# Attention over compressed blocks: one full transpose and a 128-row values product in place of two narrow transposes and a 32-row product

## The chip, the cores and the metric

The kernel runs on one core of one Trainium2 chip. The metric is the device time of one execution in microseconds. It was measured in three runs of the kernel before, and one further execution was profiled.

## The reference, cut to what matters

One layer of a decoder block: a projection of the normalized input is split into attention inputs, a state space mixer (S5) and gates; attention and S5 are gated, summed and projected; an MLP follows. 256 tokens, 2048 channels, all in fp32. The attention has 16 heads of 128 channels in four groups that share keys and values, and three branches: compressed blocks (15 of them, padded to 16), selected blocks and a sliding window.

```python
s_c = jnp.einsum('bqgrd,bngd->bgrqn', qb, kc)
p_c = masked_softmax(s_c, cmp_end[None, :] <= t[:, None])
o_c = jnp.einsum('bgrqn,bngd->bqgrd', p_c.astype(vc.dtype), vc)
...
return gb[..., 0:1] * o_c + gb[..., 1:2] * o_s + gb[..., 2:3] * o_w
...
y_b = y_s * jax.nn.sigmoid(y_s @ w_glu[l] + b_glu[l])
```

With 256 tokens every selected block and the whole window lie within reach, so the selected and the window branch are ordinary causal attention with keys and values of their own. The change concerns `o_c`, the product of the compressed branch's probabilities with the values `vc`.

## The kernel before, in words

**The large products.** Every weight product goes through "units". A unit loads 128x1024 weights into a `raw` tile (SyncE's queue, L210), ScalarE copies them to `hi` (`copy`, L117), VectorE subtracts to `lo` (`tt`, L120), and TensorE makes three products of each 128x128 piece (hi with hi, hi with lo, lo with hi; L315, L317, L318 in `gemm_pass`). `run_units` (L226) is the planner. For each unit i it issues the loads up to seven ahead, the hi copy, then the products of the unit two before (`SPLIT = 2`), the lo split, then due small steps, and then one or more steps of the background generators listed at L1549 ff. Each generator has a first and last unit and a number of steps, which are spread evenly. The order of issue on each engine is the order in which this program writes it; nothing is reordered afterwards.

**The stage of the change** is the GLU product (`glu_units`, marks "glu" to "out"), into which ada units are woven. `ada2_pe_units` (L985) does part of the adaLN vector as 32-column matmuls (L998) into bank T3, copied to `s` by ScalarE (L1000), turned at L1007 and reduced by VectorE at L1009. The finish of each GLU piece has Tanh on ScalarE (L1273) and two VectorE steps. The projections of the stage read `RU` and write banks A0 and A1, so A2 and A3 are free for attention.

**Attention** is the background generator `attention` (L1139), 34 steps for 16 heads. `attn_setup` (L1021) loads queries, keys, values and gates on SyncE's queue beforehand, among them the compressed values `vc` (32 rows, 512 columns, L1033) into a tile that used to hold the S5 operand `k0` (read for the last time by L862).

In the step of head h the program writes, in this order: `scores(h)` (three products, L1153 to L1155, banks T0 and T12), `turn1(h-1)` (four 128x128 transposes, L1203 and L1204, into T3, one ScalarE copy), `turn2(h-1)` (two 128x128 transposes, L1211, two transposes of 32 columns, L1213, into A2, two ScalarE copies), `exps(h)` (nine small VectorE instructions that mask, find maxima and negate them, with six ScalarE exponentials between). In the next step come `weigh(h)` (masks the compressed part, sums, reciprocal, scales; L1195 is its ScalarE half) and `values(h-1)` (five products into A3, L1222 to L1226, then one VectorE step).

Each head has one tile `P` of probabilities, 128 tokens of a half by columns: 768 columns for the selected and window branches of both token halves, and 64 for the compressed branch, 32 per half (16 used, 16 zero). The turned tile `PT` has 32 rows in its last 256 columns: tokens of half 0, then half 1. The product L1224 multiplies these 32 rows with the 32 rows of `vc`; all other products of `values` have 128 rows.

An fp32 product shows as two matmul records in the trace, a transpose as one. The profile names the tiles by region: `P`, `PT`, `m` and the attention inputs all lie in `RX`; `A` are the banks A0 to A3; `T` the others.

Of the kernel before, what the change touches and what calls it, by code (L numbers as in the profile page):

```python
# [81 lines left out]
def block_kernel(ctx, tc, cst_in, x, c, w_ada, b_ada, g_mix, w_in, w_ck2, pe_ck,  # L82
# [3 lines left out]
    nc = tc.nc  # L86
    V, A, PE = nc.vector, nc.scalar, nc.tensor
# [7 lines left out]
    def bank(tag):  # L95
        return pp_.tile([128, 512], FT, tag=tag, name=tag)
# [10 lines left out]
    def region(tag, n):  # L107
        return rp.tile([128, n], FT, tag=tag, name=tag)

    def scratch(name, shape):  # L110
        return dp.tile(shape, FT, tag=name, name=name)
# [4 lines left out]
    def copy(out, in_, scale=1.0):  # L116
        A.activation(out=out, in_=in_, func=AF.Copy, scale=scale)  # L117
# [10 lines left out]
    def stt(out, a, s, b, op0, op1):  # L128
        V.scalar_tensor_tensor(out=out, in0=a, scalar=s, in1=b, op0=op0, op1=op1)  # L129
# [7 lines left out]
    ident = cst[:, 0:128]  # L137
# [38 lines left out]
    d_vc = scratch("d_vc", [32, 512])  # L176
# [842 lines left out]
    at = {}  # L1019

    def attn_setup():  # L1021
        r = region("RX", 16384)
        at["r"] = r
        at["q"] = r[:, 0:4096].rearrange("p (h t) -> p h t", h=16)
        at["v"] = r[:, 4096:6144].rearrange("p (t s n) -> p t s n", t=2, s=2)
        at["K"] = r[:, 6144:8256].rearrange("p (g n) -> p g n", g=4)
        at["m"] = r[:, 8256:12352].rearrange("p (h t) -> p h t", h=16)
        at["free"] = r[:, 12352:16384]
        for i, n in enumerate(("tA", "tB")):
            at[n] = region(f"RB{i}", 4096).rearrange("p (h t) -> p h t", h=16)  # L1030
        nc.sync.dma_start(out=at["K"][:, :, 0:16], in_=d_kc.rearrange("p (g n) -> p g n", g=4))
        vc = cp.tile([128, 512], FT, tag="k0", name="vc")
        nc.sync.dma_start(out=vc[0:32], in_=d_vc)  # L1033
        at["vc"] = vc.rearrange("p (g n) -> p g n", g=4)
        for g in range(4):
            hs_ = slice(4 * g, 4 * g + 4)
            nc.sync.dma_start(out=at["q"][:, hs_, :], in_=d_q[:, hs_, :])
            for s in range(2):
                nc.sync.dma_start(
                    out=at["K"][:, g, 16:528].rearrange("p (t s n) -> p t s n", t=2, s=2)[:, :, s, :],  # L1040
                    in_=d_k[:, 4 * s + g, :].rearrange("p (t n) -> p t n", t=2))
            yield
            nc.sync.dma_start(out=at["v"][:, :, :, 128 * g:128 * g + 128], in_=d_v[:, :, :, 128 * g:128 * g + 128])
            nc.sync.dma_start(out=at["tA"][:, hs_, :], in_=d_g[:, hs_, :])
            yield
            yield
# [91 lines left out]

    def attention():  # L1139
        fa = at["free"]  # L1140
        P = [fa[:, 832 * i:832 * i + 832] for i in range(2)]
        PT = [fa[:, 1664:2688]] * 2
        sm = [fa[:, 2688 + 32 * i:2720 + 32 * i] for i in range(2)]
        for i in range(2):
            V.memset(P[i][:, 768:832], 0.0)
        q, K, vv, m = at["q"], at["K"], at["v"], at["m"]

        S = {}
# [9 lines left out]
        def exps(h):  # L1158
            S0, S1 = S["s"]
            p, s_ = P[h % 2], sm[h % 2]  # L1160
            mx, nm, su, mb = s_[:, 0:6], s_[:, 6:12], s_[:, 12:18], s_[:, 18:20]
# [20 lines left out]
        def weigh(h):  # L1182
            p, s_ = P[h % 2], sm[h % 2]
            su, cf = s_[:, 12:18], s_[:, 20:26]
            pc = p[:, 768:832].rearrange("p (i n) -> p i n", i=2)
            tt(pc[:, :, 0:16], pc[:, :, 0:16], okm, OP.mult)
            V.tensor_reduce(out=su.rearrange("p (i b) -> p i b", i=2)[:, :, 0], in_=pc[:, :, 0:16], axis=AX.X, op=OP.add)
            ts(su, su, 1e-30, OP.max)
            V.reciprocal(out=cf, in_=su)
            tt(cf.rearrange("p (i b) -> p i b", i=2), cf.rearrange("p (i b) -> p i b", i=2),  # L1190
               gates[:, :, 3 * h:3 * h + 3], OP.mult)
            for i in range(2):
                ts(pc[:, i, 0:16], pc[:, i, 0:16], cf[:, 3 * i:3 * i + 1], OP.mult)
            for s in range(2):
                A.activation(out=p[:, 128 * s:128 * s + 128], in_=p[:, 128 * s:128 * s + 128], func=AF.Copy,  # L1195
                             scale=cf[:, 1 + s:2 + s])
                ts(p[:, 256 + 256 * s:512 + 256 * s], p[:, 256 + 256 * s:512 + 256 * s], cf[:, 4 + s:5 + s], OP.mult)

        def turn1(h):
            p, o = P[h % 2], PT[h % 2]  # L1200
            ps = bank("T3")
            for s in range(2):
                PE.transpose(ps[:, 256 * s:256 * s + 128], p[:, 128 * s:128 * s + 128], ident)  # L1203
                PE.transpose(ps[:, 256 * s + 128:256 * s + 256], p[:, 256 + 256 * s:384 + 256 * s], ident)  # L1204
            copy(o[:, 0:512], ps)

        def turn2(h):
            p, o = P[h % 2], PT[h % 2]
            ps = bank("A2")
            for s in range(2):  # L1210
                PE.transpose(ps[:, 128 * s:128 * s + 128], p[:, 384 + 256 * s:512 + 256 * s], ident)  # L1211
            for i in range(2):
                PE.transpose(ps[0:32, 256 + 128 * i:384 + 128 * i], p[:, 768 + 32 * i:800 + 32 * i], ident)  # L1213
            copy(o[:, 512:768], ps[:, 0:256])
            copy(o[0:32, 768:1024], ps[0:32, 256:512])

        def values(h):
            g = h // 4
            o = PT[h % 2]
            ps = bank("A3")  # L1220
            hd = slice(128 * g, 128 * g + 128)
            PE.matmul(out=ps[:, 0:256], lhsT=vv[:, 0, 0, hd], rhs=o[:, 0:256], start=True, stop=False, skip_group_check=True)  # L1222
            PE.matmul(out=ps[:, 0:256], lhsT=vv[:, 0, 1, hd], rhs=o[:, 256:512], start=False, stop=False, skip_group_check=True)
            PE.matmul(out=ps[:, 0:256], lhsT=at["vc"][0:32, g, :], rhs=o[0:32, 768:1024], start=False, stop=False, skip_group_check=True)  # L1224
            PE.matmul(out=ps[:, 128:256], lhsT=vv[:, 1, 0, hd], rhs=o[:, 512:640], start=False, stop=False, skip_group_check=True)
            PE.matmul(out=ps[:, 128:256], lhsT=vv[:, 1, 1, hd], rhs=o[:, 640:768], start=False, stop=True, skip_group_check=True)  # L1226
            stt(m[:, h, :], at["tA"][:, h, :], 1.0, ps[:, 0:256], OP.add, OP.mult)

        for h in range(NH + 1):
            if h < NH:  # L1230
                scores(h)
            if h:
                turn1(h - 1)
                turn2(h - 1)
            if h < NH:
                exps(h)
            yield
            if h < NH:
                weigh(h)
            if h:  # L1240
                values(h - 1)
            yield
# [264 lines left out]
    with tc.manual_schedule():  # L1507
# [39 lines left out]
        def at_(name, f, nxt):  # L1547
# [16 lines left out]
            dict(name="mat1", gen=s5_matrices(1), start=marks["gb"] + CM0, end=marks["gb"] + CM1, total=4, tick=True),  # L1564
            dict(name="outs", gen=s5_outputs(), start=at_("gb", SCAN_END, "glu") + 1, end=marks["glu"] - 1, total=17),
            dict(name="load", gen=attn_setup(), start=marks["glu"] + AS0, end=marks["glu"] + AS1, total=13),
            dict(name="tb", gen=load_tb(), start=marks["glu"] + TB0, end=marks["glu"] + TB1, total=4, tick=True),
            dict(name="attn", gen=attention(), start=marks["glu"] + ATTN_WAIT, end=marks["out"] - 2, total=34),
        ]
        run_units(bgs)  # L1570
# [47 lines left out]
```

## Time and profile before

| | |
|---|---|
| median of three runs | 1780.44 us |
| lowest and highest run | 1776.47 and 1782.63 us |
| profiled execution, its own time | 1776.92 us |
| span of that execution | 1775.1 us |
| mean granted TensorE clock | 0.989 |

The span runs from the first to the last instruction of the profiled execution. PE is TensorE's matmuls, PEld its weight loads, DVE VectorE, ACT ScalarE, POOL GpSimd, SP SyncE. A duration of a matmul reaches from its start to its end in a pipeline, so durations overlap, and the distance of two starts is what a matmul costs in a stream. "Idle before" is the time in which an engine had nothing running, with the instruction that ended it; "issue" means that nothing in the profile released it.

### The profile page before, as it was taken

The page shows a single profiled execution, that of the slowest core. Times are in us where ns is not written, and L with a number is a line of the kernel's source. Part 1 is how long each engine was busy: PE and PEld are TensorE (multiplying, and loading weights), DVE is VectorE, ACT ScalarE, POOL GpSimd, SP SyncE. Part 2 cuts the span into 40 slices and gives each one's busy share as a digit, 9 for nine tenths or more (in the row PEclk, how much of TensorE's full clock was granted, in tenths as well). Part 3 has the DMA queues.
Part 4 walks back from the last instruction along what each step waited for, and adds up shares of the span by engine and source line. Part 5 has one row for each costly group of instructions (what it writes and reads, how often), then busy time and mean ns, then how long its engine had stood idle before and what let it go on. Part 6 is the DMA issues. An engine that isn't in the chain of part 4 may idle for free.

```text
span 1775.1 us, 37647 instructions
## 1 busy us (share of the span) xinstructions
PE 1718.9 (97%) x15710; PEld 1620.6 (91%) x15710; DVE 1108.5 (62%) x2032; ACT 856.3 (48%) x1379; POOL 29.4 (2%) x51
## 2 busy tenths in 40 slices
PE   6999999999999999999999999999999999999997
PEld 4788898789999988888899999999999999999997
DVE  4868468347888966666656575555555555565554
ACT  3433443754333477655544454444444544464444
POOL 1000000300000000000000000000000000000000
PEclk8999999999999999999999999999999999999998
DMA  9988756858888867876667567777777565556662
GB/s 349 327 275 315 260 180 206 267 160 296 274 274 283 254 211 243 296 244 211 214 198 262 176 219 235 235 227 224 240 234 227 179 183 184 181 176 184 184 181 81
DMA packets 121802, 406.26 MB, mean 229 GB/s; under 512 B 13904, under 2 KB 18480, under 8 KB 120864
## 3 DMA queue, kind: packets, MB, share of 16 engines
q1 hardware_dynamic: 114480, 385.49, 67.1%
q10 hardware_dynamic: 5408, 9.75, 1.5%
q0 software_dynamic: 1744, 8.62, 1.4%
q8 instruction: 123, 2.02, 0.4%
q14 instruction: 47, 0.39, 0.1%
HBM read 384.84 MB, written 16.88 MB: 226 GB/s over the span
## 4 chain that ended last, share of the span: by engine, by line
PE 87%; DVE 5%; ACT 4%; DMA 2%; issue 1%; ACTq 0%; SPq 0%; DVEq 0%
PE A L315 25%; PE A L317 24%; PE A L318 24%; PE T L998 2%; DVE lo L120 2%; PE T L343 2%; ACT hi L117 1%; ACT RX L117 1%; DMA raw<-in_l_ada_dram 1%; PE T L809 1%; PE A L897 1%; DMA raw<-in_l_vals_dram 1%; PE A L899 1%; PE A L898 1%; PE T L737 0%
## 5 line engine op out<-in xcount | busy, mean ns | idle before, releaser
L120 DVE TENSOR_TENSOR lo<-raw,hi 128x1024 fp32r<-128x1024 f32 (+1 forms) x497 | 607.0, 1223 | 507.8 <-ACT hi L117 504.0
L117 ACT ACTIVATE hi<-raw 128x1024 fp32r<-128x1024 f32 (+1 forms) x497 | 523.1, 1055 | 580.5 <-PE A L317 539.0
L315 PE MATMUL A<-RU,hi 128*128 128x256 f32 x2560 | 740.2, 289 | 3.3 <-ACT hi L117 1.5
L318 PE MATMUL A<-RU,lo 128*128 128x256 f32 x2560 | 728.0, 284 | 1.5 <-DVE lo L120 1.5
L317 PE MATMUL A<-RU,hi 128*128 128x256 f32 x2560 | 727.8, 284 | 0.0
L315 PEld LDWEIGHTS A<-RU,hi 128*128 128x128 f32 x2560 | 494.3, 193 | 27.7 <-issue 20.9
L318 PEld LDWEIGHTS A<-RU,lo 128*128 128x128 f32 x2560 | 494.4, 193 | 2.0 <-DVE lo L120 1.9
L317 PEld LDWEIGHTS A<-RU,hi 128*128 128x128 f32 x2560 | 494.7, 193 | 0.3 <-DVE RU L129 0.2
L315 PE MATMUL A<-RB,hi 128*128 128x256 f32 x1280 | 363.9, 284 | 1.4 <-ACT RB L117 1.2
L317 PE MATMUL A<-RB,hi 128*128 128x256 f32 x1280 | 362.6, 283 | 0.2
L318 PE MATMUL A<-RB,lo 128*128 128x256 f32 x1280 | 362.2, 283 | 0.0
L315 PEld LDWEIGHTS A<-RB,hi 128*128 128x128 f32 x1280 | 245.7, 192 | 3.4 <-ACT RB L117 1.6
L317 PEld LDWEIGHTS A<-RB,hi 128*128 128x128 f32 x1280 | 245.7, 192 | 0.6 <-DVE RB L129 0.5
L318 PEld LDWEIGHTS A<-RB,lo 128*128 128x128 f32 x1280 | 245.6, 192 | 0.0
L117 ACT ACTIVATE RB<-RX 128x256 fp32r<-128x256 f32 x160 | 64.3, 403 | 27.4 <-DVE RX L129 27.4
L120 DVE TENSOR_TENSOR RX<-A,RX 128x512 f32<-128x512 f32 x60 | 40.4, 687 | 30.2 <-PE A L318 29.2
L129 DVE SCALAR_TENSOR_TENSOR s<-raw,cond,s 128x1024 f32<-128x1024 f32 x45 | 57.6, 1279 | 0.1
L117 ACT ACTIVATE RX<-T 128x256 f32<-128x256 f32 (+2 forms) x81 | 39.8, 638 | 35.8 <-PE T L1204 26.6
L120 DVE TENSOR_TENSOR RB<-RX,RB 128x256 fp32r<-128x256 f32 x128 | 53.4, 418 | 1.6 <-ACT RB L117 1.6
L343 PE MATMUL T<-raw,cond 128*32 128x256 f32 x512 | 40.8, 413 | 10.0 <-DMA raw<-in_l_ada_dram 10.0
L998 PE MATMUL T<-raw,cond 128*32 128x128 f32 x1280 | 43.2, 276 | 2.0 <-ACT RX L117 2.0
L998 PEld LDWEIGHTS T<-raw,cond 128*32 128x32 f32 x1280 | 32.5, 109 | 8.4 <-ACT RX L117 4.2
(237 smaller groups left out, 1248.1 us busy)
## 6 DMA issues: line engine op xcount, KB each, us to landing
raw<-in_l_ada_dram SPq DMA_DIRECT2D x144, 512.0 KB, 4.9
raw<-in_w_in_dram SPq DMA_DIRECT2D x144, 512.0 KB, 4.6
raw<-in_w_up_dram SPq DMA_DIRECT2D x128, 512.0 KB, 4.2
raw<-in_w_down_dram SPq DMA_DIRECT2D x128, 512.0 KB, 4.5
raw<-in_w_ada_dram SPq DMA_DIRECT2D x48, 512.0 KB, 4.1
raw<-in_w_glu_dram SPq DMA_DIRECT2D x32, 512.0 KB, 5.1
raw<-in_w_out_dram SPq DMA_DIRECT2D x32, 512.0 KB, 5.8
raw<-in_l_keys_dram SPq DMA_DIRECT2D x16, 512.0 KB, 4.4
```

Source lines behind the costliest of these rows:

```text
L117: A.activation(out=out, in_=in_, func=AF.Copy, scale=scale)
L120: V.tensor_tensor(out=out, in0=a, in1=b, op=op)
L129: V.scalar_tensor_tensor(out=out, in0=a, scalar=s, in1=b, op0=op0, op1=op1)
L315: PE.matmul(out=o, lhsT=w.hi[:, at], rhs=xh, start=first and j % 2 == 0, stop=False, skip_group_check=True)
L317: PE.matmul(out=o, lhsT=w.hi[:, at], rhs=xl, start=False, stop=False, skip_group_check=True)
L318: PE.matmul(out=o, lhsT=w.lo[:, at], rhs=xh, start=False, stop=last, skip_group_check=True)
L343: PE.matmul(out=ps[q:q + 32, :], lhsT=cond[:, t0 + t:t0 + t + 1].to_broadcast([128, 32]), rhs=r[:, t, :], start=t0 == 0, stop=t0 == 12, ti ...
L809: PE.matmul(out=ps[h][:, (w * 2 + r_) * 128:(w * 2 + r_) * 128 + 128], lhsT=bl[c4 // 2][64 * h:64 * h + 64, (gw + w) % 16, r_, :], rhs=stk ...
L897: PE.matmul(out=o, lhsT=xh, rhs=u.hi[:, at], start=kt == 0, stop=False)
L898: PE.matmul(out=o, lhsT=xl, rhs=u.hi[:, at], start=False, stop=False)
L899: PE.matmul(out=o, lhsT=xh, rhs=lo[:, at], start=False, stop=kt == 15)
L998: PE.matmul(out=ps[q:q + 32, 0:128], lhsT=cond[:, kt:kt + 1].to_broadcast([128, 32]), rhs=r[:, kt % 8, :], start=kt < 4, stop=kt >= 12, ti ...
```

## The change

The compressed values are loaded twice, into rows 0 to 31 and rows 32 to 63 of `vc`, and the other rows are set to zero. `P` gets 64 more zero columns, so that its last 128 columns can be turned by one full transpose. Of the result, rows 0 to 31 hold half 0's probabilities and rows 32 to 63 half 1's. ScalarE copies the former to columns 768 to 895 of `PT`, and VectorE the latter to rows 32 to 63 of columns 896 to 1023; the rest of these 256 columns was set to zero once. The product with `vc` then has 128 rows. The VectorE copy is written at the end of `turn2`, ahead of `exps` of the next head.

```diff
         vc = cp.tile([128, 512], FT, tag="k0", name="vc")
-        nc.sync.dma_start(out=vc[0:32], in_=d_vc)
+        nc.gpsimd.memset(vc, 0.0)
+        for i in range(2):
+            nc.sync.dma_start(out=vc[32 * i:32 * i + 32], in_=d_vc)
...
-        P = [fa[:, 832 * i:832 * i + 832] for i in range(2)]
-        PT = [fa[:, 1664:2688]] * 2
-        sm = [fa[:, 2688 + 32 * i:2720 + 32 * i] for i in range(2)]
+        P = [fa[:, 896 * i:896 * i + 896] for i in range(2)]
+        PT = [fa[:, 1792:2816]] * 2
+        sm = [fa[:, 2816 + 32 * i:2848 + 32 * i] for i in range(2)]
         for i in range(2):
-            V.memset(P[i][:, 768:832], 0.0)
+            V.memset(P[i][:, 768:896], 0.0)
+
+        V.memset(PT[0][:, 768:1024], 0.0)
...
             for s in range(2):
                 PE.transpose(ps[:, 128 * s:128 * s + 128], p[:, 384 + 256 * s:512 + 256 * s], ident)
-            for i in range(2):
-                PE.transpose(ps[0:32, 256 + 128 * i:384 + 128 * i], p[:, 768 + 32 * i:800 + 32 * i], ident)
+            PE.transpose(ps[:, 256:384], p[:, 768:896], ident)
             copy(o[:, 512:768], ps[:, 0:256])
-            copy(o[0:32, 768:1024], ps[0:32, 256:512])
+            copy(o[0:32, 768:896], ps[0:32, 256:384])
+            V.tensor_copy(out=o[32:64, 896:1024], in_=ps[32:64, 256:384])
...
-            PE.matmul(out=ps[:, 0:256], lhsT=at["vc"][0:32, g, :], rhs=o[0:32, 768:1024], start=False, stop=False, skip_group_check=True)
+            PE.matmul(out=ps[:, 0:256], lhsT=at["vc"][:, g, :], rhs=o[:, 768:1024], start=False, stop=False, skip_group_check=True)
```

## Rows read from the trace of the kernel before

**Rows 1.** The page's first part: busy time of each engine, its share of the span and its instructions.

```profile
PE 1718.9 (97%) x15710; PEld 1620.6 (91%) x15710; DVE 1108.5 (62%) x2032; ACT 856.3 (48%) x1379; POOL 29.4 (2%) x51
```

**Rows 2.** TensorE's waits between 705 and 905 us: the waiting line, who ended the wait, us in total, times, the longest.

```profile
PE T L998 <- ACT RX L117: 2.0, 8, 0.3
PE T L1203 <- ACT RX L1195: 1.4, 1, 1.4
PE A L1222 <- ACT RX L117: 1.0, 3, 0.5
PE T L1007 <- ACT s L117: 0.7, 1, 0.7
```

**Rows 3.** TensorE in order of time, the values product of head 10 and what follows it: start, length, engine, line, operation.

```profile
834.14 0.60 PE L1222 MATMUL A<-RX 128*128 128x256 f32 x2
834.57 0.59 PE L1223 MATMUL A<-RX 128*128 128x256 f32 x2
835.10 0.69 PE L1224 MATMUL A<-RX,vc 32*128 32x256 f32 x2
835.72 0.49 PE L1225 MATMUL A<-RX 128*128 128x128 f32 x2
836.05 0.39 PE L1226 MATMUL A<-RX 128*128 128x128 f32 x2
836.27 0.62 PE L1153 MATMUL T<-RX 128*128 128x272 f32 x2
```

**Rows 4.** Weight loads of the values products between 720 and 905 us, grouped by line: count, busy time, mean ns of one, idle time before them and its releasers.

```profile
L1226 PEld LDWEIGHTS A<-RX 128*128 128x128 f32 x32 | 5.1, 201 | 0.0
L1225 PEld LDWEIGHTS A<-RX 128*128 128x128 f32 x32 | 5.0, 195 | 5.6 <-issue 5.6
L1224 PEld LDWEIGHTS A<-RX,vc 32*128 32x128 f32 x32 | 4.9, 190 | 5.6 <-issue 5.0 <-ACT RX L1174 0.7
```

**Rows 5.** TensorE in order of time, the end of the turn of head 10 and what follows it.

```profile
837.95 0.27 PE L1204 MATMUL T<-cst,RX 128*128 128x128 f32 x1
...
838.27 0.38 PE L1213 MATMUL A<-cst,RX 128*32 128x128 f32 x2
838.91 1.08 PE L998 MATMUL T<-raw,cond 128*32 128x128 f32 x32 [0.25 <-ACT RX L117]
```

**Rows 6.** Groups by line and form: ScalarE's copy of the compressed part, and VectorE's one copy of 128x128 out of PSUM.

```profile
L117 ACT ACTIVATE RX<-A 32x256 f32<-32x256 f32 x16 | 5.8, 361 | 0.0
...
L440 DVE COPY cols<-A 128x128 f32<-128x128 f32 x1 | 0.3, 291 | 4.7 <-PE A L439 4.7
```

**Rows 7.** VectorE, ScalarE and TensorE in order of time from 850 to 890 us, those rows that mark the steps. VectorE's rows are the first step of exps of heads 12, 13, 14 and 15. ScalarE's: the first instruction behind the exponentials of heads 12 and 13 (854.43, 863.19), the scaling of weigh of heads 12, 14 and 15 (L1195), the last read of the exponentials of head 15 (885.00). TensorE's: the 32-column transposes that end the turn of heads 11, 13 and 14 (L1213), the first transpose of the turn of heads 12 to 15 (L1203).

```profile
850.19 0.45 DVE L120 TENSOR_TENSOR T<-T,cst 128x272 f32<-128x272 f32 x1 [1.02 <-PE T L1153]
859.02 0.44 DVE L120 TENSOR_TENSOR T<-T,cst 128x272 f32<-128x272 f32 x1
873.33 0.44 DVE L120 TENSOR_TENSOR T<-T,cst 128x272 f32<-128x272 f32 x1
881.43 0.44 DVE L120 TENSOR_TENSOR T<-T,cst 128x272 f32<-128x272 f32 x1
...
854.43 0.25 ACT L117 ACTIVATE s<-T 128x128 f32<-128x128 f32 x1
857.94 0.69 ACT L1195 ACTIVATE RX<-RX 128x128 f32<-128x128 f32 x2 [2.31 <-DVE RX L120]
863.19 0.25 ACT L117 ACTIVATE s<-T 128x128 f32<-128x128 f32 x1
880.35 0.69 ACT L1195 ACTIVATE RX<-RX 128x128 f32<-128x128 f32 x2 [2.31 <-DVE RX L120]
885.00 0.21 ACT L1178 ACTIVATION_READ_ACCUMULATOR RX<-T,RX 128x1 f32 x1
888.46 0.69 ACT L1195 ACTIVATE RX<-RX 128x128 f32<-128x128 f32 x2 [2.31 <-DVE RX L120]
...
851.54 0.38 PE L1213 MATMUL A<-cst,RX 128*32 128x128 f32 x2
859.64 0.27 PE L1203 MATMUL T<-cst,RX 128*128 128x128 f32 x1
873.27 0.33 PE L1203 MATMUL T<-cst,RX 128*128 128x128 f32 x1 [0.20 <-DVE ada L1009]
873.98 0.38 PE L1213 MATMUL A<-cst,RX 128*32 128x128 f32 x2
880.81 0.33 PE L1203 MATMUL T<-cst,RX 128*128 128x128 f32 x1
881.63 0.38 PE L1213 MATMUL A<-cst,RX 128*32 128x128 f32 x2
889.72 0.27 PE L1203 MATMUL T<-cst,RX 128*128 128x128 f32 x1
```

**Rows 8.** One stretch of the table by windows: from and to, its length, busy us (and instructions) of PE, PEld, DVE, ACT, POOL, the granted clock of TensorE, DMA share, GB/s.

```profile
740.00:760.00 20.00, 19.48 (x139) 16.44 (x137) 14.44 (x43) 11.36 (x37) 0.00 (x0) 0.83 0.59 197
```

**Rows 9.** GpSimd's memsets of 128x1024 in a group; SyncE's issue of the load of `vc`, in order of time; and the wait of the issue behind it, from the waits of SyncE's queue between 690 and 725 us.

```profile
L698 POOL MEMSET s<- 128x1024 f32 x2 | 1.9, 962 | 43.9 <-DVE RX L120 43.9
...
709.84 0.69 SPq L1033 DMA_DIRECT2D vc<-d_vc  x1
...
SPq L1037 <- DMA raw<-in_w_glu_dram: 1.9, 1, 1.9
```

## The prediction, as it was put on record before the changed kernel ran

> **What bounds the kernel now.** I read the page's busy times first, then TensorE's waits in the stage that the change touches (about 720 to 900 us of the span), then that stage in order of time on each engine. TensorE is busy for 97% of the span, VectorE for 62% [rows 1]. So a stop or a saved slot on TensorE moves the end, unless ScalarE or VectorE are late in that place. TensorE's longest waits in the stage [rows 2] are few, some 5 us in 200, but they decide this case: eight of the ada products and three of the values for ScalarE's copy of the turned probabilities, one of 1.4 us for the weighing (L1195), one for the staged ada sums (L1007).
>
> **The values product.** Five products per head go to bank A3. In head 10 they start at 834.14, 834.57, 835.10, 835.72 and 836.05, and the next work starts at 836.27 [rows 3]. Two products of the same width with 128 rows follow each other after 0.43 us (834.14 to 834.57). The step into the 32-row product takes 0.53, the step out of it 0.62, and the 128-wide L1225 takes 0.33 where L1226 takes 0.22. That is 0.10 + 0.19 + 0.11 = 0.40 us per head above an even row of products. The cause shows in the weight loads: those of L1224 and L1225 stand idle for 5.6 us each over 16 heads, 0.35 at each border, with no releaser but "issue" [rows 4]; a load of 128 rows behind a product of 128 rows has no such gap (L1226, 0.0). With 128 rows in L1224 both borders vanish, while the matmul itself streams the same 256 columns. So **-0.40 us per head, 16 x 0.40 = -6.4 us gross**.
>
> [...]
>
> **The turn.** Two transposes of 32 columns become one of 128. Three of 128 columns start within 0.32 us (837.95 to 838.27), and two of 32 last 0.38 together where one transpose lasts 0.27 [rows 5]: 0.11 apart in either width. So 0.11 us per head leaves TensorE, 1.8 us gross. But in eleven heads the next instruction behind the turn waits for ScalarE's copy of the first four transposes (838.91, 0.25 us idle, one of eight; three more at L1222 [rows 2, 5]); there the slot only becomes waiting. Five heads (0, 2, 13, 14, 15) go on with projections: -0.55 us gross.
>
> **The copies.** ScalarE's copy of 32x256 (361 ns [rows 6]) becomes 32x128; that relieves it of between nothing and half, and I take nothing, as no step below waits for it. VectorE gets a new copy of 32x128 out of PSUM; its nearest row is 128x128 out of PSUM, 291 ns [rows 6]. By itself 16 x 0.29 = 4.7 us on an engine that is busy 62% of the span. What matters is its place: it stands in the queue **ahead of exps(h)**, and it waits for the turn of head h-1. Until now exps(h) waited only for scores(h), which TensorE does before the turn. Behind the copy are queued the nine steps of exps(h), then the lo split of the next unit, then weigh(h). ScalarE's exponentials wait for exps, its hi copy and Tanh stand behind those, and the turn of head h waits for weigh(h).
>
> Where VectorE comes late to exps(h) the copy costs its own 0.2 to 0.3 us. Where VectorE comes early, it now waits for the last transpose. Exps takes 3.78 us from its first step to ScalarE's last (881.43 to 885.21 [rows 7]). From the last transpose's start to the first step of exps I take 0.51, an estimate: 0.27 for the transpose and 0.24 for the signal and most of the copy; the ends are 0.27 (the copy costs nothing) and 0.27 + 0.29 + 0.1.
>
> In the middle of the stage this is mostly absorbed: VectorE is early in heads 5, 6, 7, 10, 11 and 12 (there 850.19 against a turn that ends behind 851.54 [rows 7]), its exponentials end some 1.3 us later, but before the next turn both engines wait for TensorE again (the idle VectorE has ahead of scores, such as 1.02 us at 850.19 [rows 7]). It is not absorbed in these places:
> - **Start, to 739.17.** TensorE waits 1.4 us there for the weighing of head 1 [rows 2]. The larger memsets (three of 128 to 256 columns instead of two of 64; by the copy of 128 columns, 291 ns [rows 6], between 0 and 0.9 more; I take 0.3, as a memset reads nothing) and the first copy (0.2) lie on that chain: +0.5, and what head 0 saved is lost.
> - **Heads 7 and 9.** The L1007 wait of 0.7 [rows 2] hangs on exps(8): +0.2, and the turn of head 8 follows its weighing without slack, so head 7's 0.40 is lost. The turn of head 10 follows its weighing as closely as that of head 12 does (below); the 1.3 us use that up, so head 9's 0.40 is lost too.
> - **Heads 11 to 15**, worked out from [rows 7], each "now" to "then", on one scale that starts at 850 (the full transpose starts where the first narrow one did):
>  exps(12) 850.19 to 851.54 + 0.51 = 852.05; the exponentials end at 855.8 instead of 854.4, so the weighing goes from 857.94 to 859.34, and the turn needs 0.46 behind that (880.35 to 880.81): 859.80 against 859.64. Head 11's 0.40 is gone.
>  exps(13) 859.02 to 859.80 + 0.71 + 0.51 = 861.0 (0.71 from the first to the last transpose, as at 873.27 to 873.98); the exponentials end at 864.7 instead of 863.2, +1.5. From here ScalarE and VectorE run in a chain to the reduce that frees the bank for the turn (its releaser at 873.27): 873.27 to 874.77.
>  exps(14) 873.33 to 873.98 + 1.5 + 0.51 = 875.99, +2.66; weighing 880.35 to 883.01, turn 880.81 to 883.47.
>  exps(15) 881.43 to 881.63 + 2.66 + 0.51 = 884.80, +3.37; weighing 888.46 to 891.83, turn 892.28 instead of 889.72: +2.56. With head 15's own 0.40 + 0.11 the stage leaves this part at **+2.05**.
>
> **Setup.** One memset of 128x512 on GpSimd: by the row 128x1024, 962 ns, about 0.5 us [rows 9]. Its tile is last read by L862, in the stage before, and GpSimd's queue is empty, so it is done before SyncE reaches the load at 709.8. One more load of 64 KB costs SyncE an issue of 0.69 us; the issue behind it waits 1.9 us for a weight transfer anyway [rows 9]. Behind it stand the loads of queries, keys and values and the weights. Ends: 0 (within that wait) and +0.69 (all of it reaches the weights); I take 0, as the nearest row is that wait.
>
> **Sum.** Values of heads 1 to 6, 8, 10: 8 x 0.40 = -3.2; turn of head 2: -0.1; start +0.5; head 8 +0.2; heads 11 to 15 +2.05: **-0.55 us**. Behind the stage TensorE is the bound again, so the shift is carried to the end. The sum stands against the profiled execution's 1776.92 us (span 1775.1), giving 1776.4. That execution lies 3.5 us below the median of the three runs shown (1780.44), so for the median I say 1779.9. A measurement of this kernel can tell about 0.3%, 5.3 us, from no change.
>
> **Rivals.**
> *The copy is covered* (0.23). If VectorE's wait does not reach TensorE at all, the gross gains stay: -6.4 - 0.55, less head 0 (0.51) and the +0.5 of the start: -5.9, that is 1774.5, faster by over 0.3%. For it: SPLIT lets two units lie between the split and its product, and TensorE hardly waits in the middle. Against it: the last five heads have no slack in the rows.
> [...]
> [...]
>
> **How the numbers follow.** The forecast with one clock stretch more or less has 0.55, the rivals 0.23, 0.13 and 0.05, and 0.04 is left for what I don't see. Faster by over 0.3% (below 1775.1): 0.23, the covered case. Slower (above 1785.8): 0.13 and half of the rest, 0.15. Within: 0.62. The range takes in the covered case at 1774.5 and reaches to 1786, where the forecast with one stretch more and the load's 0.69 us (1784.0) still lies inside and the second stretch does not; the runs shown spread over 6 us themselves.
>
> **What would show it.** Right: in the profile after, L1224 has no "issue" idle and the five products of a head take 1.73 us instead of 2.13; the new VectorE copy stands behind PE's turn in the waits with 5 to 10 us in all; TensorE has new waits of over 1 us at L1007 or L1203 near 871 to 885. [...]

## The result, and the profile after

The changed kernel takes **1788.67 us** (median of five runs, 1787.38 to 1791.06), the kernel before 1780.44 beside it (five runs, 1776.47 to 1782.63). The ratio is 1.0053 with an interval of 1.0037 to 1.0070: slower by 0.53%, some 9.4 us (the medians lie 8.2 us apart). The forecast was no difference, with 1779.9 us; the time lies above its range, which reached to 1786.

The profiled execution took 1791.06 us, with a span of 1789.3 and a mean granted clock of 0.984. Before the stage of the change begins, it is already 5.5 us later than the one of before (first product of the scores at 727.23 against 721.71). That lateness is older than the change: the last product of the stage before (L862) starts at 702.8 against 697.4, and the change's memset and loads come behind it (703.2 and 715.4). From that product to the first scores it is 24.3 us before and 24.4 after, and 24.3 to 24.6 in all nine kernels of this study. So I compare the stage alone, from the first scores to the values product of the last head:

| kernel | to the scores of pass 12 | from there to the last values | stage | ratio to before |
|---|---|---|---|---|
| before | 127.82 | 43.93 | 171.75 | |
| changed | 130.19 | 50.34 | 180.53 | 1.0053 |
| e1 copy behind exps | 127.99 | 42.88 | 170.87 | 0.9999 |
| e2 both copies on ScalarE | 123.95 | 43.58 | 167.53 | 0.9983 |
| e3 full rows only | 123.81 | 43.18 | 166.99 | 0.9974 |
| e4 VectorE's copy only | 129.13 | 49.61 | 178.74 | 1.0046 |
| e5 copy out of bank A3 | 128.33 | 47.58 | 175.91 | 1.0032 |
| e6 copies without a wait | 124.94 | 43.83 | 168.77 | 0.9986 |
| e7 copy out of a bank of the scores | 127.31 | 48.41 | 175.72 | 1.0022 |

(Stages are of one execution each, in us; ratios are of repeated runs, and 0.001 is 1.8 us.) A stage also holds what its execution lost to a lower granted clock, an estimate from the table of windows of 20 us (in each, 20 us times what the granted clock lacks to 1.00): 3.4 us before, 5.2 changed, 1.8 in e1, e2 and e6, 0 in e3 and e4, 3.4 in e5, 3.6 in e7; so the ratios decide, and the stages show where. The stage grew by 8.8 us, 6.4 of them in the last four heads. Behind it nothing changes: from the last values to the end of the span it is 881.6 us before and 881.5 after.

The values product did what was forecast. In order of time on TensorE, the same product as in [rows 3] (with the heads counted from 0 it is that of head 9, there called head 10):

```profile
840.58 0.60 PE L1226 MATMUL A<-RX 128*128 128x256 f32 x2
841.01 0.59 PE L1227 MATMUL A<-RX 128*128 128x256 f32 x2
841.44 0.59 PE L1228 MATMUL A<-RX,vc 128*128 128x256 f32 x2
841.87 0.38 PE L1229 MATMUL A<-RX 128*128 128x128 f32 x2
842.10 0.39 PE L1230 MATMUL A<-RX 128*128 128x128 f32 x2
842.32 0.62 PE L1157 MATMUL T<-RX 128*128 128x272 f32 x2
```

From 840.58 to 842.32 it is 1.74 us, where 2.13 were. The idle time of the weight loads at the two borders, 5.6 us each in [rows 4], is down to 1.5 and 1.1 in the groups by line, 725 to 911 us, near the 1.0 of a border between two full products (L1227):

```profile
L1229 PEld LDWEIGHTS A<-RX 128*128 128x128 f32 x32 | 6.7, 208 | 1.1
L1227 PEld LDWEIGHTS A<-RX 128*128 128x128 f32 x32 | 6.3, 198 | 1.0
L1228 PEld LDWEIGHTS A<-RX,vc 128*128 128x128 f32 x32 | 6.3, 201 | 1.5 <-DVE RX L1219 0.6
```

What took the gain and more is in TensorE's waits, 705 to 920 us, the answer to [rows 2]:

```profile
PE T L1207 <- ACT RX L1199: 7.0, 4, 2.5
PE T L1007 <- ACT s L117: 4.9, 3, 2.2
PE T L998 <- ACT RX L117: 2.9, 8, 0.4
PE A L1226 <- ACT RX L117: 1.4, 3, 0.6
PE T L1207 <- ACT s L117: 1.3, 1, 1.3
```

The turn's wait for the weighing (L1207, formerly L1203) rose from 1.4 to 7.0 us, the one at L1007 from 0.7 to 4.9. Behind both stands one line of VectorE's waits, 720 to 920 us, and it names ScalarE, not TensorE. Before, the wait ahead of exps was one for the scores; the first line is of before, the second of the changed kernel:

```profile
DVE T L120 <- PE T L1153: 2.9, 3, 1.0
...
DVE RX L1219 <- ACT RX L117: 15.7, 10, 2.8
```

The second is the new copy. Pass 12 in order of time shows it, TensorE's last two transposes, then ScalarE, then VectorE, the place of [rows 7] at 850.19:

```profile
859.20 0.38 PE L1215 MATMUL A<-cst,RX 128*128 128x128 f32 x2
859.42 0.27 PE L1216 MATMUL A<-cst,RX 128*128 128x128 f32 x1
...
859.40 0.60 ACT L117 ACTIVATE RX<-T 128x512 f32<-128x512 f32 x1 [3.03 <-PE T L1208]
859.90 0.52 ACT L117 ACTIVATE RX<-A 128x256 f32<-128x256 f32 x2
...
860.45 0.28 DVE L1219 COPY RX<-A 32x128 f32<-32x128 f32 x1 [2.82 <-ACT RX L117]
860.76 0.45 DVE L120 TENSOR_TENSOR T<-T,cst 128x272 f32<-128x272 f32 x1
```

The last transpose is over at 859.69. VectorE's copy starts at 860.45, when ScalarE's two copies out of the same bank have ended (859.90 + 0.52 = 860.42). From the last transpose's start to the first step of exps it is 860.76 - 859.42 = **1.34 us**, and so it is in heads 13, 14 and 15 (869.23 to 870.57, 885.05 to 886.39, 895.14 to 896.48). The prediction took 0.51. The written program says why: this copy waits for two engines there. In e7 (below), which reads another bank into the same place, it waits for one.

```
changed  L1219 COPY RX<-A  32x128  waits PE, Activation
e7       L1221 COPY RX<-T  32x128  waits PE
```

So the program keeps these two engines apart at bank A2, though both only read it; the trace agrees in that VectorE's copy starts 0.03 us behind the end of ScalarE's second copy (860.45 against 860.42). What this wait is for, and what happens when two engines do read the bank at once, no run here shows.

The clock, from the table by windows, the answer to [rows 8]: from and to, length, busy us (and instructions) of PE, PEld, DVE, ACT, POOL, the granted clock, DMA share, GB/s.

```profile
740.00:760.00 20.00, 17.07 (x107) 15.08 (x106) 14.76 (x43) 10.93 (x33) 0.00 (x0) 0.91 0.66 217
800.00:820.00 20.00, 17.54 (x171) 15.89 (x172) 13.33 (x39) 10.80 (x35) 0.00 (x0) 0.98 0.63 234
820.00:840.00 20.00, 19.28 (x204) 17.10 (x204) 12.03 (x43) 8.87 (x30) 0.00 (x0) 0.94 0.60 204
880.00:900.00 20.00, 15.17 (x92) 13.62 (x93) 12.34 (x45) 9.64 (x32) 0.56 (x1) 0.91 0.58 202
```

Three stretches at a lower level in place of one: in windows of 1 us the granted clock is 0.50 from 748 to 750, from 820 to 822 and from 895 to 897, and before from 742 to 748. By the windows of 20 us that is an estimated 20 x (0.09 + 0.02 + 0.06 + 0.09) = 5.2 us lost, where before lost 20 x 0.17 = 3.4. Each of the three follows a stop of TensorE of over 2 us (2.30 us up to 745.41, 2.10 up to 817.61, 2.50 up to 893.88); one of 2.24 us, up to 882.05, is followed by none (1.00 from 882 to 893).

### The profile page after: what moved, and what is told of

The parts are those of the page before. It is cut to its first block, busy times and chain, and to the rows that moved or that the text cites. A ratio compares the mean times of both kernels' runs of the same rounds, so it can differ in the third digit from the quotient of the medians.

```text
span 1789.3 us, 37647 instructions
## 1 busy us (share of the span) xinstructions
PE 1719.8 (96%) x15694; PEld 1626.3 (91%) x15694; DVE 1114.0 (62%) x2049; ACT 855.7 (48%) x1379; POOL 30.0 (2%) x52
## 4 chain that ended last, share of the span: by engine, by line
PE 85%; DVE 6%; ACT 5%; DMA 3%; issue 1%; ACTq 0%; SPq 0%; DVEq 0%
PE A L315 25%; PE A L317 24%; PE A L318 24%; DVE lo L120 2%; PE T L998 2%; PE T L343 1%; ACT hi L117 1%; ACT RX L117 1%; DMA raw<-in_l_ada_dram 1%; PE T L809 1%; PE A L897 1%; DMA raw<-in_l_vals_dram 1%; PE A L899 1%; PE A L898 1%; PE T L867 1%
## 5 line engine op out<-in xcount | busy, mean ns | idle before, releaser
L117 ACT ACTIVATE hi<-raw 128x1024 fp32r<-128x1024 f32 (+1 forms) x497 | 523.1, 1055 | 579.7 <-PE A L317 540.2
L117 ACT ACTIVATE RB<-RX 128x256 fp32r<-128x256 f32 x160 | 64.3, 403 | 27.4 <-DVE RX L129 27.4
L117 ACT ACTIVATE RX<-T 128x256 f32<-128x256 f32 (+2 forms) x81 | 39.7, 636 | 25.4 <-PE T L1208 15.7
```

## The experiments

The theories, in the order in which they came up. A, the place: VectorE's copy stands ahead of exps and waits, and that delays the exponentials and the next turn. B, the work: it is the added time on VectorE and ScalarE. C, the clock: new stops of TensorE that bring more stretches at the lower level, or a fuller product that brings the clock down. Behind the first four runs A was narrowed, and in the expectations of e5 and e7 it says: what the prediction lacked is the wait for ScalarE's copies in the same bank, and its wait for the transposes was sized rightly. Its rival D says: the place ahead of exps costs the most of it, even if the copy waits for the transposes alone.

**e1, the copy behind exps.** Written in `late(h - 1)`, called after `exps(h)`:

```diff
+            S["c"] = ps
+
+        def late(h):
+            o, ps = PT[h % 2], S["c"]
             V.tensor_copy(out=o[32:64, 896:1024], in_=ps[32:64, 256:384])
...
+            if h:
+                late(h - 1)
```

> The changed kernel with VectorE's new copy written behind exps of the next head instead of ahead of it; all else stays. Theory A (the place of the copy in VectorE's queue is the cause: it waits for ScalarE's two copies out of the same bank, ends 1.34 us behind the last transpose's start, and exps, hi, lo, weigh and the next turn follow): the values product keeps its 1.73 us per head, TensorE's waits in the stage fall from 18.4 us back to 5 to 7, and the kernel is 5 to 7 us faster than the one before the change: ratio 0.996 to 0.998. Rival B (the work that was added costs: VectorE's 16 x 0.28 us, the memsets, the second load): nothing of that is gone, so it stays near 1.005. Rival C (TensorE's clock falls because of the fuller product): it stays at or above 1.003 with granted clocks below 1.00 in the stage.

Measured: 0.9999 (0.9990 to 1.0008), 1778.52 us. The loss is gone, so the place carries it. The gain that was expected is missing, and the waits of TensorE show where it went:

```profile
PE A L1232 <- DVE RX L1223: 4.0, 3, 2.4
PE A L1232 <- issue: 1.5, 1, 1.5
```

In heads 0 to 3 the values product (L1232 is the product with `vc` here) follows so soon that it stands for the copy, which now comes late: 4.0 us in three heads, and 1.5 in head 0, where the profile names no releaser but the copy ends at 734.14 and the product starts at 734.24.

**e2, both copies on ScalarE.** No copy on VectorE.

```diff
-            V.tensor_copy(out=o[32:64, 896:1024], in_=ps[32:64, 256:384])
+            copy(o[32:64, 896:1024], ps[32:64, 256:384])
```

> The changed kernel with the second copy of the compressed part on ScalarE too, so VectorE has no copy there; ScalarE makes 256, 128 and 128 columns instead of 256 and 256. Theory A: 5 to 6 us faster than the kernel before (ratio 0.997), a little behind the copy on VectorE behind exps, as ScalarE has some 0.25 us more per head. Rival B, if VectorE's added work is the cost: about 4 us of the 8 come back, ratio 1.002 to 1.003. Rival C: at or above 1.003.

Measured: 0.9983 (0.9973 to 0.9993), 1775.23 us: a gain of 3.0 us, less than the 5 to 6 that were expected and about half of what the prediction's covered case gave (5.9 us).

**e3, full rows only.** To the kernel before: `vc` and the last columns of `PT` are zeroed, and the product reads 128 rows; the narrow transposes and ScalarE's one copy stay.

```diff
+        nc.gpsimd.memset(vc, 0.0)
...
+        V.memset(PT[0][:, 768:1024], 0.0)
...
-            PE.matmul(out=ps[:, 0:256], lhsT=at["vc"][0:32, g, :], rhs=o[0:32, 768:1024], start=False, stop=False, skip_group_check=True)
+            PE.matmul(out=ps[:, 0:256], lhsT=at["vc"][:, g, :], rhs=o[:, 768:1024], start=False, stop=False, skip_group_check=True)
```

> The kernel before with one part of the change alone: the product with the compressed values has 128 rows, rows 32 to 127 of both operands are set to zero once; the two narrow transposes and ScalarE's one copy stay, VectorE has no copy. Theory A: the product gains 0.40 us per head, less what waits for ScalarE and VectorE anyway: 5 to 6.5 us faster, ratio 0.9965 to 0.997. Rival C (the 128-row product itself costs, by clock or by weight loads that are not hidden): 1.000 or above.

Measured: 0.9974 (0.9963 to 0.9986), 1773.29 us, the fastest of all, ahead of both kernels; 4.6 us, a little less than expected. Over these runs the mean granted clock was 0.9884, and 0.9878 in the kernel before, so some 1 us of the 4.6 may be the clock; in the two profiled stages it is 3.4 of 4.8. TensorE in order of time, the product of [rows 3] again, and then the groups of the weight loads, 720 to 905 us:

```profile
832.31 0.60 PE L1224 MATMUL A<-RX 128*128 128x256 f32 x2
...
834.05 0.62 PE L1155 MATMUL T<-RX 128*128 128x272 f32 x2
```

```profile
L1227 PEld LDWEIGHTS A<-RX 128*128 128x128 f32 x32 | 6.1, 190 | 0.8
L1226 PEld LDWEIGHTS A<-RX,vc 128*128 128x128 f32 x32 | 6.1, 190 | 0.8
```

1.74 us for the five products and 0.8 us of idle at either border, with nothing changed but the rows: the 32 rows were what cost 0.40 us per head on TensorE. In that form the block-diagonal tile is not needed; zeros below the 32 rows do.

**e4, VectorE's copy only.** To the kernel before: ScalarE copies half of the compressed part and VectorE the other half, in the place of the change, still 32 rows.

```diff
-            copy(o[0:32, 768:1024], ps[0:32, 256:512])
+            copy(o[0:32, 768:896], ps[0:32, 256:384])
+            V.tensor_copy(out=o[0:32, 896:1024], in_=ps[0:32, 384:512])
```

> The kernel before with VectorE's copy alone: ScalarE copies half 0 of the compressed part and VectorE half 1, in the place where the change has it, ahead of exps; the 32-row product and the narrow transposes stay. Theory A: the whole loss without the gain, 8 + 6 = 14 us slower, ratio 1.006 to 1.009; TensorE's waits in the stage 15 us or more. Rival B (VectorE's own 0.28 us per head, the rest being setup): under 4.5 us, ratio below 1.0025. Rival C: no change.

Measured: 1.0046 (1.0032 to 1.0060), 1786.9 us. Below what was expected, because I had added the parts up (the change's loss and the gain that it hides): the copy alone costs as much as the whole change. The waits of VectorE, then those of TensorE:

```profile
DVE RX L1216 <- ACT RX L117: 16.3, 10, 3.2
```

```profile
PE T L1203 <- ACT RX L1195: 5.3, 5, 2.1
PE T L1007 <- ACT s L117: 3.5, 3, 1.7
```

The same waits as in the changed kernel. And the clock is not needed for it: the stage takes 7.0 us longer than before with the granted clock at 1.00 in every 20 us from 720 to 900, though before lost 3.4 us there to the lower level.

**e5, the copy out of bank A3.** The full transpose is written a second time, into A3, and VectorE reads there.

```diff
+            pd = bank("A3")
+            PE.transpose(pd[:, 0:128], p[:, 768:896], ident)
...
-            V.tensor_copy(out=o[32:64, 896:1024], in_=ps[32:64, 256:384])
+            V.tensor_copy(out=o[32:64, 896:1024], in_=pd[32:64, 0:128])
```

> The changed kernel, with the full transpose of the compressed part done twice, the second time into bank A3, from which VectorE's copy reads; in the written program this copy then waits for TensorE alone and no longer for ScalarE's two copies out of A2. Its place ahead of exps stays. Theory A (what was missing in the prediction is the wait for ScalarE's copies, 0.83 us per pass: 1.34 instead of 0.51 us from the last transpose's start to exps): the stage from the first scores to the last values takes 171 to 174 us as the recorded sum has it (before 171.75, changed 180.53), ratio 0.999 to 1.001; VectorE's waits at the copy fall from 15.7 us to 5 to 9. Rival D (the place alone is the cause, the wait for the transposes is enough): the stage stays above 177 us and the ratio at 1.003 or above.

Measured: 1.0032 (1.0021 to 1.0043), 1783.94 us. By the ratio that is what was said for D (1.003 or above), by the stage, 175.91, for neither; and the run doesn't decide, as A3 is the bank of the values product, which now waits for the copy in its turn, 3.1 us:

```profile
PE A L1228 <- DVE RX L1221: 3.1, 3, 1.5
```

**e6, copies without a wait.** As e2, but in the copy's place VectorE makes two copies of the same size from a constant into columns that nothing reads.

```diff
-            V.tensor_copy(out=o[32:64, 896:1024], in_=ps[32:64, 256:384])
+            copy(o[32:64, 896:1024], ps[32:64, 256:384])
+            V.tensor_copy(out=at["free"][0:32, 2944:3072], in_=cst[0:32, 0:128])
+            V.tensor_copy(out=at["free"][0:32, 3072:3200], in_=cst[0:32, 0:128])
```

> The changed kernel with both copies of the compressed part on ScalarE (as measured above, 0.9983), and in the place of VectorE's copy two copies of 32x128 of a constant into an unused part of the region, which wait for nothing. Theory A (it is the wait, not VectorE's time): 0 to 1.5 us over 0.9983, ratio 0.998 to 0.9995; TensorE's waits in the stage as there. Rival B (VectorE's occupied time counts): 16 x 0.4 us come on top, ratio 1.001 or above.

Measured: 0.9986 (0.9976 to 0.9996), 1776.65 us, against e2's 0.9983: twice 207 ns per head on VectorE, in that very place, cost nothing that can be measured (the copy that they stand for takes 284 ns). Theory B falls.

**e7, the copy out of a bank of the scores.** As e5, but the second transpose goes into the last 128 columns of the bank that the next scores wrote just before, which no ScalarE copy of the turn reads.

```diff
+            pd = S["s"][0] if h < NH - 1 else bank("T0")
+            PE.transpose(pd[:, 384:512], p[:, 768:896], ident)
...
+            V.tensor_copy(out=o[32:64, 896:1024], in_=pd[32:64, 384:512])
```

> As the run with the copy's own bank, but the second full transpose goes into the unused columns of the bank of the scores (T0) instead of A3, so that the values product doesn't wait for VectorE's copy to give A3 back (3.1 us of TensorE's waits there). VectorE's copy stays ahead of exps and waits for TensorE alone. Theory A (the recorded chain of waits is right and only its step from the last transpose to exps was too short: 0.51 against 1.34 us): with a step of 0.6 to 0.7 us and 0.11 us per head for the second transpose, the stage takes 171 to 174 us (before 171.75, changed 180.53, copy's own bank 175.91), ratio 0.999 to 1.001. Rival D (the place ahead of exps costs more than that chain says, whatever it waits for): 175 us or more, ratio 1.002 or above.

Measured: 1.0022 (1.0013 to 1.0031), 1782.12 us, stage 175.72: just inside what was said for D (1.002 and 175 or more), outside what was said for A. So the wait for ScalarE is not the whole. Pass 12 in order of time, TensorE and VectorE, then VectorE's wait at the copy:

```profile
856.54 0.27 PE L1218 MATMUL T<-cst,RX 128*128 128x128 f32 x1
...
856.86 0.28 DVE L1221 COPY RX<-T 32x128 f32<-32x128 f32 x1 [2.20 <-PE T L1218]
857.17 0.45 DVE L120 TENSOR_TENSOR T<-T,cst 128x272 f32<-128x272 f32 x1
```

```profile
DVE RX L1221 <- PE T L1218: 9.5, 9, 2.2
```

Without ScalarE in the bank the step takes 857.17 - 856.54 = 0.63 us instead of 1.34, and more than half of the loss is gone (3.9 us are left of 9.4). What stays is the wait for the transposes. So the ratios split the change in three: without any wait (e6) 0.9986, that is -2.5 us; the wait for the transposes (e7 less e6) 0.0036, +6.4 us, of which e7's own second transposes may be up to 16 x 0.11 = 1.8; the wait for ScalarE's copies (the change less e7) 0.0031, +5.5 us. In all +9.4. By the intervals of the ratios each of the two differences is uncertain by some 2 to 3 us.

The last difference is not the wait alone. The mean granted clock was 0.985 over the runs of the change and 0.988 over those of e6 and of e7; at 1.8 us for a thousandth up to 4.7 of the 5.5 us can have gone through the clock. What the traces show without it is the step: 1.34 - 0.63 = 0.71 us in each of heads 12 to 15, some 2.8 us. How much of the rest is the lower level behind the longer stops stays open.

## Why the prediction was wrong, by its own steps

**The step that failed: "From the last transpose's start to the first step of exps I take 0.51", with ends of 0.27 and 0.66.** It measured 1.34, outside both ends. I counted what the copy waits for among the instructions that write its source, and not those that read the same bank. With a bank to itself it is 0.63, inside the ends, and the estimate would have stood. The 0.83 too few come back in each of heads 12 to 15: 4 x 0.83 = 3.3 us on a chain that the prediction had traced rightly (exps, exponentials, weighing, turn). It gave these heads +2.05, which is +2.45 up to the start of the last values, as head 15's own product comes behind it; the stretch from the scores of pass 12 to there grew by 50.34 - 43.93 = 6.4. Of the 4.0 between, 3.3 are this step, and the stretch at the lower clock near 895 is 1.8; together they are a little more than is to be explained, and I can't part them further. By the ratios the wait in the bank is worth +5.5 us with the clock's share in it (above), where the sum had 0.

**"Mostly absorbed" in the middle.** The forecast had +0.2 at L1007 near head 8 and nothing for head 3. In the profile after, in order of time, TensorE stands at both places, and longer than forecast at the start:

```profile
745.41 0.33 PE L1207 MATMUL T<-cst,RX 128*128 128x128 f32 x1 [2.30 <-ACT RX L1199]
...
767.25 0.33 PE L1207 MATMUL T<-cst,RX 128*128 128x128 f32 x1 [1.34 <-ACT s L117]
...
817.61 0.66 PE L1007 MATMUL T<-cst,s 128*128 128x128 f32 x4 [2.10 <-ACT s L117]
```

2.30 where 1.38 + 0.5 was said, 1.34 where nothing was, 2.10 where 0.7 + 0.2 was. The late exponentials delay ScalarE's copy of the ada sums (`s`, L117), which is queued behind them.

**The tail, ahead of the turns of heads 13 and 14: right in place, too small in size.** Stops of about 1.7 us were forecast near 871 and 882, which is near 879 and 890 here, as pass 12 begins 7.9 us later. Ahead of the turn of head 13 there are 2.24 (at L1007, the ada transposes just before it) and 0.28, ahead of that of head 14 there are 2.50: each some 0.8 more than forecast, about the missing 0.83 of the step. A stop of 1.11 ahead of the turn of head 12 was not named:

```profile
868.41 0.33 PE L1207 MATMUL T<-cst,RX 128*128 128x128 f32 x1 [1.11 <-ACT RX L1199]
882.05 0.66 PE L1007 MATMUL T<-cst,s 128*128 128x128 f32 x4 [2.24 <-ACT s L117]
884.34 0.33 PE L1207 MATMUL T<-cst,RX 128*128 128x128 f32 x1 [0.28 <-DVE ada L1009]
893.88 0.33 PE L1207 MATMUL T<-cst,RX 128*128 128x128 f32 x1 [2.50 <-ACT RX L1199]
```

**The values product, -0.40 us per head: right** as a price on TensorE (1.74 against 2.13). The chance of 0.05 was for a full load that waits as well, and that is out: the loads of L1228 have 1.5 us of idle in all, 0.6 of it behind the copy, in place of the 5.6.

**The covered case, -5.9 us: too much.** Free of the wait, e2, e3 and e6 gain 3.0, 4.6 and 2.5 us. The table shows where a part of the rest stays: in the last four heads these kernels take 43.58, 43.18 and 43.83 against 43.93, a gain of 0.1 to 0.75 us, where the case had counted 0.40 for each of four products and 0.11 for each of three turns, 1.9 in all. There the turn follows the weighing without slack, by the prediction's own [rows 7]; a shorter product on TensorE only lengthens the wait for ScalarE and VectorE (ahead of the turn of head 14 TensorE waits 0.81 us for the weighing in e2, 0.48 in e3 and 0.84 in e6, where it waited for nothing before). The case ought to have left heads 11 to 14 out. Where the remainder stays is not shown.

**Waiting for the transposes: about right.** The prediction's sum and its covered case lie 5.35 us apart; e7 and e6 lie 6.4 apart, with e7's own second transposes in it. It is the larger of the two waits by the ratios, as D had it, and the sum had counted it.

So against the sum of -0.55: the bank's wait +5.5, the smaller gain of the case without a wait +3.4 (1.8 of it in the last four heads), and +1.05 on the wait for the transposes make the +9.4 that were measured.

**The clock: one part, whose size stays open.** The chance of 0.13 was for two more stretches at the lower level, of 3.4 us each, and the range left room for one. No run shows that a new stop costs 3.4 us: in the stage of the profiled execution there are two stretches more, but all three are shorter, an estimated 1.6 to 1.8 us each and together 1.8 us more than before. Over the five runs the mean granted clock was 0.984 to 0.987; in the sets of e1 to e4 the kernel before had 0.985 to 0.991. A thousandth of the span is 1.8 us, so up to some 5 us of the loss could go through the clock, in the stage or out of it. What speaks against the clock as the cause is e4, which loses 8.2 us with 1.00 throughout the stage of its profiled execution and a mean of 0.985 to 0.989 over its runs. Whether and when a stop brings the lower level isn't settled (below).

**Setup at 0: right.** With one load or two, the first scores come 24.3 to 24.6 us behind the last product of the stage before.

## What to carry to other kernels

In this program VectorE's copy out of a PSUM bank waited for ScalarE's copies out of the same bank, and no longer did when it read another one (1.34 us from the last transpose's start to exps, then 0.63): when a copy is split over two engines, look in the written program whether they take turns, and give each its own bank. Before something is put into the queue of an engine with time to spare, look at what stands behind it there and at all that it waits for; the price is that wait, and here sixteen copies of 0.28 us, 4.5 us together, cost 11.9 us (the change against e6, the clock's share included) by waiting in front of exps, while copies in the same place without a wait cost nothing that can be measured. A slot saved on the busiest engine counts only in those passes in which it is the last to be ready (in the last four heads e2, e3 and e6 gained 0.1 to 0.75 us, where 1.9 had been counted), so count the passes before you multiply.

## What the runs showed of the hardware that was not expected

The product over 32 rows among products over 128 cost more than a product over 128 rows: 0.40 us per head at its borders (2.13 against 1.74 us for the five), with the columns unchanged. Full rows, padded with zeros, took it away in the change and in e3 alike.

Not every stop of TensorE was followed by the lower clock. In e3, in order of time on TensorE, then by windows:

```profile
740.73 0.33 PE L1205 MATMUL T<-cst,RX 128*128 128x128 f32 x1 [1.76 <-ACT RX L1197]
...
742.45 0.70 PE L1224 MATMUL A<-RX 128*128 128x256 f32 x2 [0.52 <-ACT RX L117]
```

```profile
740.00:760.00 20.00, 18.30 (x152) 16.52 (x152) 14.71 (x43) 11.99 (x37) 0.00 (x0) 1.00 0.70 221
```

Stops of 1.76 and 0.52 us, and the granted clock stays at 1.00; before, stops of 1.4 and 0.5 in the same place were followed by 0.83 [rows 2, 8]. e4, with 1.57 and 0.52 there, kept 1.00 too; e2, with 1.86 and 0.63, had 0.91: the five products behind them take 3.34 us there (744.31 to 747.65), and 1.76 in e3 (742.45 to 744.21). What decides between them no run here shows.
